# Score products of a gated linear recurrence in 32-column tiles instead of 128-column ones

## The chip, the cores and the metric

The kernel runs on one core of a Trainium2 chip. Time is device time in microseconds (us) of one execution; a lower time is better. The core has a matrix engine (TensorE, in the profile PE for the matmuls and PEld for the loads of the stationary operand), VectorE (DVE), ScalarE (ACT), GpSimd (POOL) and queues that start DMA transfers (SP among them). Each engine works through its own queue in order and waits on semaphores for the others. Matmul results land in PSUM, eight banks of 512 fp32 columns by 128 partitions, from where VectorE or ScalarE copies them to SBUF.

## What is computed

The reference is one layer of a decoder trunk for 1024 tokens plus 16 meta tokens, width 1024: a wide input projection, a gated linear recurrence in four heads, a causal pooling branch, a gated sum of both, an output projection, and a gated MLP. The part that matters here is the recurrence, cut to its core:

```python
def _hgrn2_chunk_step(state, xs):
    q, k, v, lf = xs
    b = jnp.cumsum(lf, axis=2)
    o_inter = jnp.einsum('bhtk,bhkv->bhtv', q * jnp.exp(b), state)
    diff = b[:, :, :, None, :] - b[:, :, None, :, :]
    ...
    decay = jnp.where(causal, jnp.exp(jnp.where(causal, diff, 0.0)), 0.0)
    scores = jnp.einsum('bhtk,bhtsk,bhsk->bhts', q, decay, k)
    o_intra = jnp.einsum('bhts,bhsv->bhtv', scores, v)
    ...
```

For every pair of tokens t >= s the score is a product over 128 channels in which each channel has its own decay exp(b[t] - b[s]). The decay can't be pulled out of the product for all pairs at once without overflow.

## The kernel before, in words

The kernel takes chunks of 128 tokens (`NCH` = 8 of them after the 16 meta tokens) and computes the 128 x 128 score matrix of a chunk by levels. A pair t > s is handled by the level `lv` of 2, 4, 8, 16, 32, 64 in which t lies in the right half and s in the left half of the same aligned block of 2 `lv` tokens: there the decay is split at the middle of the block into a factor for q and one for k, and a plain matmul gives the score. Pairs within two neighbouring tokens come from the "pair diagonal", a matmul of k and q with one more decay factor.

All of this is the generator `head_steps(h)` (lines 570 to 733), one per head, with channels on the partitions and tokens on the free axis:

- `level_in` (581 to 593) makes the tile `d` of a level: in each block the right half holds the scaled q, the left half the scaled k (VectorE or GpSimd at 587, 591, 592; ScalarE's exponentials at 589, 590).
- `level_mm` (595 to 613) multiplies. For levels 2 to 16 a chunk is one matmul (607): all 128 tokens of `d` are the stationary operand, the 64 tokens of the right halves move, and the result is 128 partitions by 64 columns, of which only the entries within a block count. For levels 32 and 64 there is one matmul per block (603), whose stationary operand is the left half (32 or 64 columns) and whose result lies at partition 2 `lv` i of the bank. Where 2 `lv` fits into the 16 meta tokens, a small matmul does those (612).
- `level_out` (615 to 631) brings the results into the score matrix `sc`. For levels 2 to 16 it is a masked copy per chunk on VectorE (627), with `masks[lv]` choosing the entries within blocks. For levels 32 and 64 plain copies (621).
- The levels go in pairs, (2, 4), (8, 16), (32, 64): the inputs of two levels, a `yield`, then the matmuls and the copies of both (lines 634 to 639).
- The pair diagonal (676 to 683): per chunk a matmul of 128 stationary k columns with 128 moving q columns (680) into two banks of four chunks, and a masked copy per chunk (683) with `mbase`. Line 685 does it for the meta tokens.
- After that come the states between chunks (692 to 703) and the outputs, which multiply `sc` with v (719).

All these matmuls are in fp32, and each such call shows in the trace as two weight loads and two MATMULs. The projections (`proj`, lines 164 to 178) split fp32 into two reduced-precision parts and use three matmuls instead.

What sets the order: the string `ORDER` (44 to 46) interleaves the projections of the four heads (F, Q, G), of the pooling branch (PV, PP) and of the branch outputs (BB, BA) with the steps of the heads (h0 to h3, one `yield` each). It is worked through at 981 to 1007. The list `POOLED` (47 to 49) gives some elementwise operations to GpSimd. In this stage the order within each engine's queue isn't written out by hand: it is decided when the kernel is built, by a planner that simulates the engines with its own costs (line 1523). The stages before it and most of the one after it are ordered by hand (`manual_schedule`). SBUF tiles of one token row come from 24 slots (`FM_SLOTS`), PSUM banks from a pool of eight.

Of the kernel before, what the change touches and what calls it, by code (L numbers as in the profile page):

```python
# [14 lines left out]
P = 128  # L15
D = 1024
SEQ = 1024
NM = 16
# [4 lines left out]
TQ = L - T0  # L23
CW = TQ // 3
HEADS = 4
NCH = 8
FF = 2816
KF = FF // P
# [28 lines left out]
def trunk_kernel(ctx: ExitStack, tc: tile.TileContext, x, meta_tokens, mix_norm_pre,  # L57
# [4 lines left out]
    act, dve, pool_e, pe = nc.scalar, nc.vector, nc.gpsimd, nc.tensor  # L62
# [21 lines left out]
    def nm(s):  # L84
        cnt[0] += 1
        return f"{s}_{cnt[0]}"

    def slot(n, dtype=F32, name="s"):
        return stage["fm", "p"].tile([P, n], dtype, tag="fm", name=nm(name), padded_shape=[P, L])
# [4 lines left out]
    def bank(name="ps"):  # L94
        return stage["ps", "p"].tile([P, 512], F32, tag="ps", name=nm(name))
# [11 lines left out]
    def small(shape, name, tag, bufs=4):  # L107
        return sm.tile(shape, F32, tag=tag, name=nm(name), bufs=bufs)
# [272 lines left out]
    CQ, CF, CI, CG, CV, CA, CB = 0, 512, 1024, 1536, 2048, 2560, 3584  # L381
    row_tiles = [(0, NM)] + [(NM + P * i, P) for i in range(NCH)]

# [19 lines left out]
    prow = slot(P, name="prow")  # L403
    NPR = 4 * KF + 3 * HEADS
    for at, n, src in ((0, 3 * KF, ffn_conv_w[0].rearrange("j (f p) -> (j f) p", p=P)),
                       (3 * KF, KF, ffn_conv_b[0].rearrange("(f p) -> f p", p=P)),
                       (4 * KF, HEADS, hgrn_lower_bounds[0].rearrange("(h p) -> h p", p=P)),
                       (4 * KF + HEADS, HEADS, hgrn_out_norm[0].rearrange("(h p) -> h p", p=P)),
                       (4 * KF + 2 * HEADS, HEADS, pool_scale[0].rearrange("(h p) -> h p", p=P))):
        nc.sync.dma_start(prow[at : at + n], src)  # L410
    par = const.tile([P, NPR], F32, name="par")
    cvw = par[:, : 3 * KF].rearrange("p (j f) -> p j f", j=3)
    cvb = par[:, 3 * KF : 4 * KF]
    lbt, ong, psc = (par[:, 4 * KF + i * HEADS : 4 * KF + (i + 1) * HEADS] for i in range(3))

    lb = const.tile([P, HEADS], F32, name="lb")
    oml = const.tile([P, HEADS], F32, name="oml")
# [80 lines left out]

    vd = dram.tile([NCH, P, 512], F32, name="vscr")
    vmeta = const.tile([P, 512], F32, name="vmeta")  # L500

    LEVELS = (2, 4, 8, 16, 32, 64)
    masks = {}
    mbase = const.tile([P, P], U8, name="mbase")
# [65 lines left out]
    def head_steps(h):  # L570
        q, kk, b, lf = (heads[h][z] for z in ("q", "kk", "b", "f"))
        heads[h]["v"] = slot(NCH * P, name="vh")
        nc.sync.dma_start(heads[h]["v"].rearrange("p (c v) -> p c v", c=NCH),
                          vd[:, :, h * P : (h + 1) * P].rearrange("c p v -> p c v"))
        sc = slot(NCH * P, name="sc")
        scm = small([NM, NM], "scm", "scm", 2)
# [17 lines left out]

        def level_mm(lv, qk):
            ps = bank("sl")
            half = lv >= 32
            for c in range(NCH):
                t = NM + c * P
                if half:  # L600
                    for i in range(P // (2 * lv)):
                        s, n = t + 2 * lv * i, 2 * lv * i
                        pe.matmul(ps[n : n + lv, c * lv : (c + 1) * lv], qk[:, s : s + lv], qk[:, s + lv : s + 2 * lv],
                                  start=True, stop=True)
                    continue
                rhs = qk[:, t : t + P].rearrange("p (b two h) -> p b two h", two=2, h=lv)[:, :, 1, :]
                pe.matmul(ps[:, c * 64 : (c + 1) * 64], qk[:, t : t + P], rhs, start=True, stop=True)
            pm = None
            if 2 * lv <= NM:
                pm = bank("sm")  # L610
                rhs = qk[:, :NM].rearrange("p (b two h) -> p b two h", two=2, h=lv)[:, :, 1, :]
                pe.matmul(pm[:NM, : NM // 2], qk[:, :NM], rhs, start=True, stop=True)
            return ps, pm

        def level_out(lv, ps, pm):
            if lv >= 32:
                o3 = sc.rearrange("p (c t) -> p c t", c=NCH)
                p3 = ps[:, : NCH * lv].rearrange("p (c h) -> p c h", c=NCH)
                for i in range(P // (2 * lv)):
                    n = 2 * lv * i  # L620
                    dve.tensor_copy(o3[n : n + lv, :, n + lv : n + 2 * lv], p3[n : n + lv])
                return
            o4 = sc.rearrange("p (c b two h) -> p c b two h", c=NCH, two=2, h=lv)[:, :, :, 1, :]
            p4 = ps.rearrange("p (c b h) -> p c b h", c=NCH, h=lv)
            m3 = masks[lv].rearrange("p (b h) -> p b h", h=lv)
            for c in range(NCH):
                dve.copy_predicated(o4[:, c], m3, p4[:, c])
            if pm is not None:
                dve.copy_predicated(scm.rearrange("p (b two h) -> p b two h", two=2, h=lv)[:, :, 1, :],
                                    masks[lv][:NM, : NM // 2].rearrange("p (b h) -> p b h", h=lv),  # L630
                                    pm[:NM, : NM // 2].rearrange("p (b h) -> p b h", h=lv))

        pend = []
        for pair in ((2, 4), (8, 16), (32, 64)):
            pend = [(lv, level_in(lv)) for lv in pair]
            yield
            outs = [(lv,) + level_mm(lv, d) for lv, d in pend]
            for o_ in outs:
                level_out(*o_)
# [26 lines left out]
        for j in range(2):  # L666
            pt = bank("pt")
            for i in range(4):
                t = NM + (4 * j + i) * P
# [3 lines left out]
        pe.transpose(pm[:NM, :P], kd[:, :NM], ident)  # L673
        ktm = small([NM, P], "ktm", "ktm", 2)
        act.copy(ktm, pm[:NM, :P])
        for j in range(2):
            ps = bank("sb")
            for i in range(4):
                t = NM + (4 * j + i) * P
                pe.matmul(ps[:, i * P : (i + 1) * P], kk[:, t : t + P], q[:, t : t + P], start=True, stop=True)  # L680
            for i in range(4):
                c = 4 * j + i
                dve.copy_predicated(sc[:, c * P : (c + 1) * P], mbase, ps[:, i * P : (i + 1) * P])
        pm = bank("sm")
        pe.matmul(pm[:NM, :NM], kk[:, :NM], q[:, :NM], start=True, stop=True)
        dve.copy_predicated(scm, mbase[:NM, :NM], pm[:NM, :NM])
# [4 lines left out]
        ps = bank("ds")  # L691
        pe.matmul(ps[:, :P], ktm, vmeta[:NM, h * P : (h + 1) * P], start=True, stop=True)
        act.copy(st[:, :P], ps[:, :P])
        for j in range(2):
            ps = bank("ds")
            cs = [c for c in range(4 * j, 4 * j + 4) if c < NCH - 1]
            for c in cs:
                i = c - 4 * j
                pe.matmul(ps[:, i * P : (i + 1) * P], kt[:, c * P : (c + 1) * P], V(c, h), start=True, stop=True)
            for c in cs:  # L700
                i = c - 4 * j
# [5 lines left out]
        o, rs = slot(TQ, name="o"), slot(TQ, name="rs")  # L707
# [6 lines left out]
        for j in range(2):  # L714
            ps = bank("po")
            for i in range(4):
                c = 4 * j + i
                t = NM + c * P
                pe.matmul(ps[:, i * P : (i + 1) * P], V(c, h), sc[:, c * P : (c + 1) * P], start=True, stop=False)
                pe.matmul(ps[:, i * P : (i + 1) * P], st[:, c * P : (c + 1) * P], qs[:, t : t + P],  # L720
                          start=False, stop=True)
# [3 lines left out]
        for lo, n in CH_Q:  # L725
            ps = bank("ms")
# [157 lines left out]
    with tc.manual_schedule(engines={E.Activation, E.DVE, E.PE}):  # L884
# [36 lines left out]
        for i in range(2, len(vtiles)):  # L921
            ps = bank("pv")
# [22 lines left out]
        for h in range(EARLY_G):  # L945
            src, n_k, xs, chunks, post = job("G", h)
            r = proj(None, 0, n_k, xs, chunks, ws=gl.next(), name="pg")
# [12 lines left out]
        for e in range(0, EARLY, 2):  # L960
            p = gates.start_pair(e)
# [343 lines left out]
    with tc.manual_schedule(engines={E.PE, E.Activation, E.DVE, E.Pool}):  # L1305
        for c in range(3):
            tiles_ = [pair("pm") for _ in range(3)]
            own = Rows(c, tiles_)
# [47 lines left out]
        p = [ffn.first(e) for e in range(EARLY)]  # L1356
# [171 lines left out]
```

## Time and profile before

| | |
|---|---|
| time, three runs | 1385.9, 1389.66, 1389.27 us; median 1389.27 |
| profiled execution, span from first to last instruction | 1388.5 us |
| instructions | 21566 |
| mean granted TensorE clock | 0.993 of full speed |
| matmuls of line 607 (levels 2 to 16), MATMULs | 256, from 287.3 to 437.5 us |
| matmuls of line 680 (pair diagonal), MATMULs | 64, from 352.5 to 479.8 us |
| masked copies of line 627 / 683 | 128 / 32 |

The profile gives for the profiled execution its span; the time of that execution with what lies around the span is not given separately, and the runs' times stand beside it. The page has the busy time of each engine, the span in 40 equal slices with the busy share in tenths, the DMA queues and the costliest groups of instructions. Other views answer questions: busy time in chosen stretches (optionally of one source line only), groups of instructions by line and shape with the mean length of one, who waited for whom, and a time line that merges equal neighbours. Matmuls are pipelined, so the lengths of successive MATMULs overlap, and what one costs the engine is the spacing between starts.

### The profile page before, as it was taken

The numbers are of one execution on the slowest core, as the hardware profiler recorded it, in microseconds if no ns is written. First come the engines' busy times: TensorE is split into PE (matmuls) and PEld (weight loads), VectorE is DVE, ScalarE is ACT, GpSimd is POOL, SyncE is SP. The second block draws the span as 40 slices with busy tenths as digits, with TensorE's granted clock in tenths as the row PEclk, the third lists the DMA queues.
The fourth block names the chain that finished last, engine by engine and source line by source line (L and its number), as shares of the span: only waits on it lengthen the run. The fifth ranks groups of instructions, "written<-read, shape, count | busy, mean of one in ns | idle before, by whom it ended". The sixth has DMA issues, their size and how long they took to land. (4 is left out here: it accounts for less than half of the span.)

```text
span 1388.5 us, 21566 instructions
## 1 busy us (share of the span) xinstructions
PE 1353.9 (98%) x8415; PEld 1225.2 (88%) x8415; DVE 961.7 (69%) x1397; ACT 564.5 (41%) x945; POOL 474.6 (34%) x357
## 2 busy tenths in 40 slices
PE   9999999999999999999987999999999999999997
PEld 7899999999999899987777788888999998788786
DVE  6764645389875755565589888888887777654557
ACT  5553333357554562136564322232222223543343
POOL 2015411237444610160037565534567652000100
PEclk9999999999999999999999999999999999999999
DMA  6134333321110024589842677665677889966524
GB/s 246 40 113 146 115 114 107 99 62 31 49 49 5 23 82 133 190 276 343 287 129 82 176 209 207 187 179 146 164 156 176 197 210 263 366 228 201 180 70 166
DMA packets 133220, 215.21 MB, mean 155 GB/s; under 512 B 8327, under 2 KB 76523, under 8 KB 133120
## 3 DMA queue, kind: packets, MB, share of 16 engines
q1 hardware_dynamic: 121056, 189.47, 40.4%
q0 software_dynamic: 12064, 24.38, 10.4%
q8 instruction: 66, 1.08, 0.3%
q14 instruction: 34, 0.28, 0.1%
HBM read 160.84 MB, written 76.05 MB: 171 GB/s over the span
## 5 line engine op out<-in xcount | busy, mean ns | idle before, releaser
L262 PE MATMUL P<-v,whi 128*128 128x258 f32 (+2 forms) x528 | 162.9, 322 | 7.0 <-DVE g L1227 4.5
L263 PE MATMUL P<-v,whi 128*128 128x258 f32 (+2 forms) x528 | 161.9, 321 | 0.0
L265 PE MATMUL P<-v,wlo 128*128 128x258 f32 (+2 forms) x528 | 141.0, 321 | 1.0 <-DVE wlo L210 1.0
L262 PEld LDWEIGHTS P<-v,whi 128*128 128x128 f32 x528 | 100.9, 191 | 15.5 <-DVE g L1227 4.9
L137 POOL TENSOR_TENSOR wlo<-wraw,whi 128x1024 fp32r<-128x1024 f32 (+2 forms) x23 | 50.0, 2173 | 183.6 <-ACT whi L136 101.8
L263 PEld LDWEIGHTS P<-v,whi 128*128 128x128 f32 x528 | 100.7, 191 | 7.6
L161 PE MATMUL pd<-rot 128*128 128x512 f32 x272 | 106.0, 390 | 0.3 <-DVE rot L1287 0.3
L162 PE MATMUL pd<-rot 128*128 128x512 f32 x272 | 105.9, 389 | 0.0
L136 ACT CAST whi<-wraw 128x1024 fp32r<-128x1024 f32 (+2 forms) x44 | 36.3, 825 | 148.1 <-PE pba L174 31.5
L265 PEld LDWEIGHTS P<-v,wlo 128*128 128x128 f32 x528 | 88.0, 190 | 8.8 <-DVE wlo L210 1.2
L209 ACT CAST whi<-wraw 128x512 fp32r<-128x512 f32 x90 | 53.0, 617 | 104.4 <-PE P L263 84.4
L210 DVE TENSOR_TENSOR wlo<-wraw,whi 128x512 fp32r<-128x512 f32 x82 | 75.7, 946 | 21.2 <-ACT whi L209 21.2
L1287 DVE TENSOR_TENSOR rot<-yt,rot 128x1024 fp32r<-128x1024 f32 x33 | 41.2, 1249 | 69.7 <-ACT rot L1286 69.7
L1171 POOL TENSOR_TENSOR ys<-y 128x512 f32<-128x512 f32 x22 | 35.2, 1599 | 143.7 <-issue 97.5
L235 POOL TENSOR_TENSOR swa<-wraw,wraw 128x512 f32<-128x512 f32 x30 | 45.1, 1503 | 96.4 <-DMA wraw<-in_w_in_dram 62.4
L160 PE MATMUL pd<-rot 128*128 128x512 f32 x272 | 72.8, 391 | 2.1 <-ACT rot L1286 2.1
L209 ACT CAST whi<-swa 128x512 fp32r<-128x512 f32 x60 | 35.8, 618 | 86.7 <-PE P L263 75.8
L1286 ACT CAST rot<-yt 128x1024 fp32r<-128x1024 f32 x33 | 34.6, 1051 | 89.2 <-PE pd L161 89.2
L1219 DVE SCALAR_TENSOR_TENSOR y<-g,par,y 128x1024 f32<-128x1024 f32 x44 | 65.7, 1494 | 0.7
L160 PEld LDWEIGHTS pd<-rot 128*128 128x128 f32 x272 | 50.8, 188 | 13.9 <-ACT rot L1286 3.4
L262 PE MATMUL P<-t2h,whi 128*128 128x258 f32 (+1 forms) x196 | 58.0, 312 | 3.7 <-ACT t2h L333 2.8
L209 ACT CAST whi<-swb 128x512 fp32r<-128x512 f32 x60 | 35.9, 619 | 63.2 <-PE P L263 62.4
(348 smaller groups left out, 4273.0 us busy)
## 6 DMA issues: line engine op xcount, KB each, us to landing
wraw<-in_w_in_dram SPq DMA_DIRECT2D x36, 512.0 KB
yt<-ysum SPq DMA_DIRECT2D x33, 512.0 KB
wraw<-in_ffn_w_gate_dram SPq DMA_DIRECT2D x26, 512.0 KB
wraw<-in_w_out_dram SPq DMA_DIRECT2D x24, 512.0 KB
wraw<-in_ffn_w_up_dram SPq DMA_DIRECT2D x22, 512.0 KB
wsum<-in_ffn_w_down_dram SPq DMA_DIRECT2D x22, 512.0 KB
ysum<-ys SPq DMA_DIRECT2D x11, 768.0 KB
sa<-sscr SPq DMA_DIRECT2D x16, 513.0 KB
```

The lines of the kernel that those rows point to most:

```text
L137: eng.tensor_tensor(lo, raw, rr(hi), ALU.subtract)
L160: pe.matmul(ps, ahi, bhi, start=first, stop=False)
L161: pe.matmul(ps, ahi, blo, start=False, stop=False)
L162: pe.matmul(ps, alo, bhi, start=False, stop=last)
L209: act.copy(hi, src)
L210: (pool_e if 4 <= i < 2 * self.early else dve).tensor_tensor(lo, src, rr(hi), ALU.subtract)
L235: pool_e.tensor_tensor(s1, a21, a22, ALU.add)
L262: pe.matmul(x[:, o : o + w], whi[:, k, :], xh[:, c : c + w], start=(k == 0), stop=False)
L263: pe.matmul(x[:, o : o + w], whi[:, k, :], xl[:, c : c + w], start=False, stop=False)
L265: pe.matmul(x[:, o : o + w], wlo[:, k, :], xh[:, c : c + w], start=False, stop=(k == 3))
L1219: dve.scalar_tensor_tensor(a, g[:, :, j : j + n], cvw[:, j, m : m + 1], a, ALU.mult, ALU.add)
L1287: dve.tensor_tensor(lo, src, rr(hi), ALU.subtract)
```

## The change

A constant `B` = 32 is added. For levels 2 to 16 and for the pair diagonal, each chunk of 128 tokens is cut into four blocks of 32, since no pair of these levels crosses a block of 32. Each block is its own matmul call: its 32 tokens are the stationary operand, and the moving operand is its 16 right-half tokens (levels) or its 32 tokens (diagonal). The result of block i lies at partitions 32 i to 32 i + 31, that is in the column tile i of the array, and the chunks stand next to each other: 16 columns per chunk for a level, 32 for the diagonal, which now takes one bank instead of two. The masked copies go per block position i, over all eight chunks at once: four copies per level, on 32 partitions and 8 x 16 elements each, and four for the diagonal, on 32 partitions and 8 x 32 elements. The mask of one chunk is broadcast over the chunks. Levels 32 and 64, the meta tokens and everything else stay.

```diff
-            half = lv >= 32
+            half = lv >= B
             for c in range(NCH):
                 t = NM + c * P
...
-                rhs = qk[:, t : t + P].rearrange("p (b two h) -> p b two h", two=2, h=lv)[:, :, 1, :]
-                pe.matmul(ps[:, c * 64 : (c + 1) * 64], qk[:, t : t + P], rhs, start=True, stop=True)
+                for i in range(P // B):
+                    own = qk[:, t + i * B : t + (i + 1) * B]
+                    rhs = own.rearrange("p (b two h) -> p b two h", two=2, h=lv)[:, :, 1, :]
+                    pe.matmul(ps[i * B : (i + 1) * B, c * B // 2 : (c + 1) * B // 2], own, rhs, start=True, stop=True)
...
-            for c in range(NCH):
-                dve.copy_predicated(o4[:, c], m3, p4[:, c])
+            n = B // 2
+            o6 = sc.rearrange("p (c i b two h) -> p c i b two h", c=NCH, i=P // B, two=2, h=lv)
+            p4 = ps[:, : NCH * n].rearrange("p (c b h) -> p c b h", c=NCH, h=lv)
+            for i in range(P // B):
+                r = slice(i * B, (i + 1) * B)
+                m4 = masks[lv][r, i * n : (i + 1) * n].rearrange("p (o b h) -> p o b h", o=1, h=lv)
+                dve.copy_predicated(o6[r, :, i, :, 1, :], m4.to_broadcast([B, NCH, n // lv, lv]), p4[r])
...
-        for j in range(2):
-            ps = bank("sb")
-            for i in range(4):
-                t = NM + (4 * j + i) * P
-                pe.matmul(ps[:, i * P : (i + 1) * P], kk[:, t : t + P], q[:, t : t + P], start=True, stop=True)
-            for i in range(4):
-                c = 4 * j + i
-                dve.copy_predicated(sc[:, c * P : (c + 1) * P], mbase, ps[:, i * P : (i + 1) * P])
+        ps = bank("sb")
+        for c in range(NCH):
+            for i in range(P // B):
+                own = slice(NM + c * P + i * B, NM + c * P + (i + 1) * B)
+                pe.matmul(ps[i * B : (i + 1) * B, c * B : (c + 1) * B], kk[:, own], q[:, own], start=True, stop=True)
+        for i in range(P // B):
+            r = slice(i * B, (i + 1) * B)
+            dve.copy_predicated(sc.rearrange("p (c i t) -> p c i t", c=NCH, i=P // B)[r, :, i, :],
+                                mbase[r, r].rearrange("p (o t) -> p o t", o=1).to_broadcast([B, NCH, B]),
+                                ps[r, : NCH * B].rearrange("p (c t) -> p c t", c=NCH))
```

More of the change, by code (lines that the diff above doesn't have):

```diff
@@ L25 @@
 HEADS = 4
+B = 32
 NCH = 8
@@ L615, in level_out @@
         def level_out(lv, ps, pm):
-            if lv >= 32:
+            if lv >= B:
                 o3 = sc.rearrange("p (c t) -> p c t", c=NCH)
@@ L622, in level_out @@
                 return
-            o4 = sc.rearrange("p (c b two h) -> p c b two h", c=NCH, two=2, h=lv)[:, :, :, 1, :]
-            p4 = ps.rearrange("p (c b h) -> p c b h", c=NCH, h=lv)
-            m3 = masks[lv].rearrange("p (b h) -> p b h", h=lv)
-            for c in range(NCH):
-                dve.copy_predicated(o4[:, c], m3, p4[:, c])
+            n = B // 2
[5 more added lines that the diff above has]
+                dve.copy_predicated(o6[r, :, i, :, 1, :], m4.to_broadcast([B, NCH, n // lv, lv]), p4[r])
             if pm is not None:
```

## The prediction

> **What bounds the kernel now.** I read the page's engine table and its slices first.
>
> ```profile
> span 1388.5 us, 21566 instructions
> ...
> PE 1353.9 (98%) x8415; PEld 1225.2 (88%) x8415; DVE 961.7 (69%) x1397; ACT 564.5 (41%) x945; POOL 474.6 (34%) x357
> ...
> PE   9999999999999999999987999999999999999997
> ...
> DVE  6764645389875755565589888888887777654557
> ```
>
> TensorE is busy for 98% of the span, without a dip from the ninth to the fourteenth slice (278 to 486 us), where the changed lines run. VectorE's digits stand at 8, 9, 8, 7 there first, then at 5. So I cut that part into two stretches, at the point where VectorE's load falls, and counted busy time in each.
>
> ```profile
> 283.00:372.00 89.00, 87.70 (x687) 85.98 (x686) 81.18 (x177) 53.33 (x81) 47.65 (x21) 1.00 0.14 43
> 372.00:483.00 111.00, 108.52 (x824) 104.97 (x823) 77.46 (x167) 56.88 (x96) 54.92 (x28) 0.98 0.09 27
> ```
>
> The columns are stretch, length, then PE, PEld, DVE, ACT and POOL busy with counts, then the granted clock. PE is idle for 1.30 us in the first stretch and 2.48 us in the second, so almost any PE work taken out shortens them, as long as nothing else then ends last. The candidate is DVE: it has 7.82 us to spare in the first stretch and 33.54 us in the second. What DVE waits for decides whether that room can be used. First stretch, all rows of its waits:
>
> ```profile
> DVE f L558 <- ACT f L557: 3.0, 2, 1.5
> DVE f L551 <- ACT f L546: 1.4, 2, 0.7
> DVE sc L627 <- PE sl L607: 1.1, 1, 1.1
> DVE wlo L137 <- ACT whi L136: 1.0, 1, 1.0
> DVE d L592 <- ACT d L590: 0.9, 1, 0.9
> DVE d L591 <- ACT d L589: 0.2, 1, 0.2
> ```
>
> Second stretch, its two longest:
>
> ```profile
> DVE sc L683 <- PE sb L680: 11.5, 3, 6.2
> DVE sc L627 <- PE sl L607: 8.5, 3, 7.0
> ```
>
> In the first stretch 6.5 us of DVE's waits are for ScalarE and 1.1 us for PE: DVE is close to a second bound there. In the second, 20.0 us are waits for the very matmuls that change: PE alone is the bound.
>
> **How much work is touched.** The matmuls of line 607 (levels 2 to 16) and 680 (pair diagonal), counted in the same two stretches:
>
> ```profile
> 283.00:372.00 89.00, 19.53 (x160) 18.81 (x160) 1.00 0.14 43
> 372.00:483.00 111.00, 11.68 (x96) 11.22 (x96) 0.98 0.09 27
> ```
>
> ```profile
> 283.00:372.00 89.00, 2.05 (x16) 1.86 (x16) 1.00 0.14 43
> 372.00:483.00 111.00, 5.85 (x48) 5.60 (x48) 0.98 0.09 27
> ```
>
> An fp32 matmul call shows as two weight loads with two MATMULs, so 16 MATMULs are one unit: one level, or the diagonal, of one head (8 chunks). There are 10 + 1 = 11 units in the first stretch and 6 + 3 = 9 in the second, 20 in all. After the change each unit has 8 x 4 = 32 calls, 64 MATMULs: 960 more in all.
>
> **The price of a MATMUL before and after.** Three bursts give it. Rows of a time line start with start and length; rows of groups end with busy time and mean length of one.
>
> ```profile
> 450.17 1.95 PE L680 MATMUL sb<-q,kk 128*128 128x128 f32 x16
> ```
>
> ```profile
> 322.29 0.18 PE L612 MATMUL sm<-d 128*16 128x8 f32 x1
> 322.30 0.22 PE L603 MATMUL sl<-d 128*32 128x32 f32 x1
> 322.33 0.17 PE L612 MATMUL sm<-d 128*16 128x8 f32 x1
> 322.35 0.67 PE L603 MATMUL sl<-d 128*32 128x32 f32 x31
> ```
>
> ```profile
> 323.12 0.98 PE L603 MATMUL sl<-d 128*64 128x64 f32 x14
> ```
>
> ```profile
> L680 PE MATMUL sb<-q,kk 128*128 128x128 f32 x64 | 7.9, 277 | 0.6 <-POOL kk L663 0.6
> L603 PE MATMUL sl<-d 128*64 128x64 f32 x64 | 4.6, 225 | 0.0
> L603 PE MATMUL sl<-d 128*32 128x32 f32 x128 | 2.9, 197 | 0.0
> ```
>
> A burst's length less its last matmul, over the number of steps, is the spacing. 128 columns: (1.95 - 0.277)/15 = 111.5 ns. 64 columns: (0.98 - 0.225)/13 = 58.1 ns. 32 columns: (0.67 - 0.197)/30 = 15.8 ns. From 128 to 64 columns the spacing halves; from 64 to 32 it falls to a quarter. The extra factor has a reason in the code: level 32 writes alternately to partitions 0 and 64, two column tiles, while level 64 writes to one. So one 32-column tile takes a matmul every 2 x 15.8 = 31.6 ns, and two run side by side. The L603 matmul that starts at 322.30, between the two halves of an L612 call, also says that a tile does not queue behind another tile's work.
>
> The change goes round four tiles. If all four run at once, the spacing is 31.6/4 = 7.9 ns; if no more than two do, it stays 15.8; without overlap it is 31.6. A unit costs 16 x 111.5 = 1.784 us before. After: 64 x 15.8 = 1.011 us (gain 0.773, for 20 units 15.5 us), 64 x 7.9 = 0.506 us (gain 1.278, in all 25.6 us), 64 x 31.6 = 2.022 us (loss 0.238, in all 4.8 us). The loss begins above 27.9 ns. No row shows four tiles. The nearest is the two-tile burst of 15.8, with the same kind of loop; overlap was full for two, so I take 12 ns, halfway towards four: 0.768 us a unit, a gain of 1.016, for 20 units 20.3 us of PE.
>
> [...]
>
> **Switching between tile widths.** Level 8's burst and the next unit of the same head:
>
> ```profile
> 303.07 1.89 PE L607 MATMUL sl<-d 128*128 128x64 f32 x16
> 304.89 0.21 PE L612 MATMUL sm<-d 128*16 128x8 f32 x2
> 305.03 0.32 PE L607 MATMUL sl<-d 128*128 128x64 f32 x1
> ```
>
> From 303.07 to 305.03 is 1.96 us, 0.18 more than a unit: the two narrow L612 matmuls and the way into and out of their width. When the neighbours are narrow too, some of the twelve such visits (levels 2, 4, 8 of four heads) lose it. Between 0 and 12 x 0.18 = 2.2 us; I take 1 us, as a change of width stays at each end of a burst.
>
> **VectorE.** Eight copies per unit become four, with as many elements per partition altogether (4 x 128 for a level, 4 x 256 for the diagonal).
>
> ```profile
> 351.17 1.13 DVE L627 COPY_PREDICATED sc<-mask,sl 128x64 f32<-128x64 uint8 x8
> 357.50 1.68 DVE L683 COPY_PREDICATED sc<-mbase,sb 128x128 f32<-128x128 uint8 x8
> ```
>
> 1.13/8 = 141 ns for 64 elements and 1.68/8 = 210 ns for 128: 1.08 ns an element and 72 ns fixed. Four fixed costs less is 0.29 us a unit, 5.8 us in all, 3.2 of them in the first stretch. That four copies use 32 partitions each saves nothing; if the longer pattern cost more per element, this saving goes, so 0 to 5.8. The copies of a unit wait for its last matmul as now. The diagonal takes one PSUM bank instead of two; no wait of this part is for a bank of it, so nothing is priced. The new instructions are fetched too (packets, MB, share of 16 DMA engines):
>
> ```profile
> q8 instruction: 66, 1.08, 0.3%
> ```
>
> 21566 instructions took 66 packets, so 1920 more take 6, at 0.003 x 16 x 1388.5/66 = 1 us each. They lie beside running matmuls and I price them at nothing; were each waited for, 6 us.
>
> **The sum.** Second stretch: 9 x 1.016 = 9.1 us; I count 9. First stretch: PE offers 11 x 1.016 = 11.2 us. DVE then needs 81.18 - 3.2 + its 6.5 us of waits for ScalarE = 84.5 of 89, which allows 4.5 us if nothing is rearranged; PE can run ahead with projections that wait for no head, so the truth is between 4.5 and 11.2, and I take 6.5, nearer the lower as in-order queues stop at the first step that is late. With 1 us of switching, 16.5 us. The profiled span of 1388.5 becomes 1372. The page gives no time around the span; the median of the runs is 1389.27, 0.77 higher, and they differ by 3.8, so I add 0.77: about 1373. This case by itself reaches from 4.5 + 9 x 0.773 = 11.5 us to 25.6 + 1 us: 1362.7 to 1377.8.
>
> **Rivals.**
> VectorE sets the pace, in the first stretch fully and in part of the second. For it: 81.18 of 89 us. Against: 20 us of DVE's waits in the second are for the matmuls that shrink. It gives 4.5 us, and half of 9 x 0.773 = 7.0: 8 us, so 1381.
>
> The gain is lost to order. Outside the blocks ordered by hand, a planner decides each engine's queue at build time, and it will see other lengths. The longest PE wait here now:
>
> ```profile
> PE ppv L173 <- ACT st L693: 2.5, 1, 2.5
> ```
>
> Six or seven more waits of 2.5 us take all 16.5: 1389. Against it: four heads' steps now cost PE 1.30 + 2.48 = 3.78 us of idle time altogether.
>
> Slower: the matmuls cannot be issued that fast. The 15.8 ns burst is 32 MATMULs long, behind slow ones during which the sequencer could fill the queue; now 64 and, for a pair of levels, 128 stand in a row. If the sequencer settles at the 58.1 ns of the 64-column burst, a unit costs 3.72 us, and 20 cost 38.7 us more: 1428; at 31.6 ns it is 1394, with the six fetches up to 1400. It decides from 27.9 ns on; just short of that, at 25 ns, a unit would cost 1.6 us and the whole would come to 1385.6. Against it: right after that burst 14 matmuls of 64 columns still came every 58.1 ns, half of what 128 columns take, so the array and not the sequencer set their pace. [...]
>
> That the four tiles give no more than two is not a rival but the lower half of my case.
>
> **Chances.** Forecast 0.53, VectorE's pace 0.20, lost to order (or a spacing of about 25 ns) 0.13, issue-bound beyond 27.9 ns 0.14, half of it at 1394 to 1400. A measurement of this kernel can tell about 0.3%, 4.2 us, from no change. The first two cases are faster, with 0.02 of the third: 0.75; within: 0.11; slower: 0.14. The range goes from 1362, all four tiles and nothing lost, to 1390, which takes in the lost gain; it leaves out the slower case and a little below.
>
> **What would show it.** MATMULs of the level line: 1024 of 32 columns in place of 256, in bursts of 64 or 128 spaced 8 to 16 ns; PE busy time in this part down by some 15 to 25 us; DVE's copies at about 0.21 us and half as many; the second stretch shorter by about 9 us and the first by 4 to 11, with DVE over 90% busy in it; everything after it as before, only earlier. Wrong: a spacing above 28 ns, or PE idle time that grows by as much as its work shrinks.

## The result and the profile after

After: median 1378.72 us of four runs (1375.45 to 1380.77), beside 1389.47 us (1385.9 to 1389.81) of the kernel before. The ratio is 0.9928, 95% interval 0.991 to 0.9945: 7.6 to 12.5 us faster. The predicted time was 1373 in a range of 1362 to 1390, so the direction and the range held, and the gain was 46 to 76% of the 16.5 us expected. The profiled execution took 1380.77 us with a span of 1379.1, 1.7 us lying around it; its span is 9.4 us shorter than before's.

The same lines of the page as before: span, busy times, TensorE's and VectorE's slices, instruction fetches.

```profile
span 1379.1 us, 23409 instructions
...
PE 1334.7 (97%) x9375; PEld 1204.7 (87%) x9375; DVE 964.0 (70%) x1317; ACT 564.8 (41%) x945; POOL 472.1 (34%) x357
...
PE   9999999998999999999988999999999999999997
...
DVE  6764645389887655555589898787878776744557
...
q8 instruction: 74, 1.21, 0.3%
```

TensorE's busy time fell by 1353.9 - 1334.7 = 19.2 us. Its idle time, span less busy time, rose from 34.6 to 44.4 us, by 9.8. The difference, 9.4 us, is what the span gained: half of what TensorE saved came back as waiting. TensorE's tenth slice now shows an 8 (310 to 345 us), where VectorE's shows a 9. The two stretches of the prediction, moved to where that work now lies (length, then PE, PEld, DVE, ACT, POOL busy, then the clock):

```profile
283.00:370.00 87.00, 76.53 (x1195) 73.64 (x1194) 80.55 (x126) 52.92 (x80) 44.55 (x21) 0.92 0.15 45
370.00:480.00 110.00, 106.54 (x1309) 102.22 (x1308) 83.45 (x140) 60.91 (x101) 55.42 (x28) 0.98 0.10 30
```

TensorE is idle for 10.47 us in the first and 3.46 in the second, where it was 1.30 and 2.48. The clock in the first fell from 1.00 to 0.92. Where the time was won is seen from two marks. The first is the first output matmul of head 0 (its row has start and length); the row under it counts all the work ahead of it. Before:

```profile
375.00 0.39 PE L712 MATMUL po<-scm,vmeta 16*128 16x16 f32 x2
```

```profile
0.00:375.00 375.00, 371.38 (x2682) 355.09 (x2683) 243.18 (x451) 174.14 (x311) 115.94 (x99) 1.00 0.32 102
```

After:

```profile
375.65 0.39 PE L719 MATMUL po<-scm,vmeta 16*128 16x16 f32 x2
```

```profile
0.00:375.65 375.65, 362.86 (x3210) 345.53 (x3210) 246.57 (x407) 173.99 (x311) 112.95 (x99) 0.98 0.32 102
```

The 528 MATMULs more are those of the eleven units ahead of the mark (704 in place of 176), so the work is the same. TensorE was busy for 8.5 us less and waited 9.2 us longer: 12.79 in place of 3.62. By then nothing was won. The changed matmuls ahead of the mark fell by more than 8.5 us. They took 19.53 us (levels) and 2.05 us (diagonal) before, the 160 and 16 MATMULs of the prediction's first stretch. After, levels and then diagonal:

```profile
0.00:375.65 375.65, 7.47 (x640) 6.93 (x640) 0.98 0.32 102
```

```profile
0.00:375.65 375.65, 0.76 (x64) 0.65 (x64) 0.98 0.32 102
```

That is 13.35 us less. So TensorE's other matmuls, the same in number, took 13.35 - 8.52 = 4.8 us longer, where the granted clock in the stretch from 283 us on was 0.92 instead of 1.00. Waiting took 9.2 us of the 13.35 and the slower other matmuls 4.8; together that is all of it.

The second mark is the last matmul of the diagonal (shortest, median and longest in ns, then first and last start). Before:

```profile
L680 PE MATMUL sb<-q,kk x64: 275/275/378, 352.5 to 479.9; 128*128 128x128 f32 x64
```

After:

```profile
L685 PE MATMUL sb<-q,kk x256: 196/196/217, 352.1 to 471.3; 128*32 128x32 f32 x128
```

There it was 8.6 us. So between the two marks 9.2 us were won, and the stretch before the first gave none. The level and diagonal matmuls themselves, groups of the stretch 270 to 490 us after (busy time, mean ns, then idle time before them and its cause):

```profile
L610 PE MATMUL sl<-d 128*32 128x16 f32 x1024 | 11.5, 189 | 5.2 <-DVE d L593 4.7 <-ACT qs L648 0.5
L685 PE MATMUL sb<-q,kk 128*32 128x32 f32 x256 | 3.1, 199 | 0.3 <-POOL kk L668 0.3
```

Together 14.6 us, and 5.5 us of waiting. What they mostly wait for is the tile `d` that VectorE makes, 4.7 us; that is just under half of TensorE's 10.47 us in the first stretch, and the longest of its other waits there, 2.2 us, is for ScalarE. Time line of TensorE after, a burst that did not wait, and one that did:

```profile
286.95 0.70 PE L610 MATMUL sl<-d 128*32 128x16 f32 x62
```

```profile
317.82 1.06 PE L610 MATMUL sl<-d 128*32 128x16 f32 x64 [3.64 <-DVE d L593]
```

The first gives a spacing of (0.70 - 0.189)/61 = 8.4 ns. The second, the same kind of burst, is half as long again: it follows 3.64 us of idleness, and the granted clock there is 0.50, as two short stretches show.

```profile
316.00:318.00 2.00, 0.18 (x12) 0.18 (x16) 2.00 (x3) 1.99 (x6) 2.00 (x2) 0.92 0.00 0
318.00:320.00 2.00, 2.00 (x146) 2.00 (x144) 2.00 (x1) 1.88 (x3) 2.00 (x2) 0.50 0.04 8
```

In the first of these VectorE, ScalarE and GpSimd are busy nearly throughout and TensorE is not: the inputs of the levels are late.

Last, VectorE's masked copies after (groups as above):

```profile
L632 DVE COPY_PREDICATED sc<-mask,sl 32x128 f32<-32x128 uint8 x64 | 21.3, 332 | 5.7 <-PE sl L610 4.2
L688 DVE COPY_PREDICATED sc<-mbase,sb 32x256 f32<-32x256 uint8 x16 | 7.1, 443 | 5.0 <-PE sb L685 4.0 <-PE sm L692 0.8
```

Before:

```profile
L627 DVE COPY_PREDICATED sc<-mask,sl 128x64 f32<-128x64 uint8 x128 | 19.6, 247 | 9.6 <-PE sl L607 9.5
L683 DVE COPY_PREDICATED sc<-mbase,sb 128x128 f32<-128x128 uint8 x32 | 7.0, 296 | 11.5 <-PE sb L680 11.5
```

Half as many copies took 28.4 us in place of 26.6.

### The profile page after: what moved, and what is told of

Same layout as the page of the kernel before. It is cut to its first block, busy times and chain, and to the rows that moved or that the text cites. A ratio compares the mean times of both kernels' runs of the same rounds, so it can differ in the third digit from the quotient of the medians.

```text
span 1379.1 us, 23409 instructions
## 1 busy us (share of the span) xinstructions
PE 1334.7 (97%) x9375; PEld 1204.7 (87%) x9375; DVE 964.0 (70%) x1317; ACT 564.8 (41%) x945; POOL 472.1 (34%) x357
## 5 line engine op out<-in xcount | busy, mean ns | idle before, releaser
L1293 ACT CAST rot<-yt 128x1024 fp32r<-128x1024 f32 x33 | 34.6, 1052 | 93.1 <-PE pd L162 93.1
L211 DVE TENSOR_TENSOR wlo<-swb,whi 128x512 fp32r<-128x512 f32 x60 | 56.8, 952 | 8.3 <-ACT whi L210 8.3
```

The costliest lines, as they stand in the source:

```text
L211: (pool_e if 4 <= i < 2 * self.early else dve).tensor_tensor(lo, src, rr(hi), ALU.subtract)
```

## The experiments

Three explanations for the missing part of the gain were tested. V: VectorE's queue became the bound, and its masked copies are what would have to shrink. O: the planner, which orders each engine's queue when the kernel is built, lost it by its new order. P, formed after the first four runs: the bound is the elementwise work that makes the level inputs, on VectorE and GpSimd together, not the copies by themselves. Each ratio is to the kernel before on the same chip, with its 95% interval. The last three columns are from the page of one profiled execution of each kernel, where TensorE's idle time is the span less its busy time; for z3 that execution was the fastest of five, for x3 the slowest of ten:

| kernel | median us | ratio (interval) | span | PE busy | PE idle |
|---|---|---|---|---|---|
| before | 1389.47 | | 1388.5 | 1353.9 | 34.6 |
| after | 1378.72 | 0.9928 (0.991 to 0.9945) | 1379.1 | 1334.7 | 44.4 |
| x1, wide, no masked copies | 1386.92 | 0.9989 (0.9978 to 1.0) | 1385.2 | 1351.0 | 34.2 |
| x2, narrow, no masked copies | 1380.22 | 0.9935 (0.9921 to 0.995) | 1378.4 | 1330.5 | 47.9 |
| x3, one tile after the other | 1385.81 | 0.9981 (0.997 to 0.9991) | 1387.2 | 1353.2 | 34.0 |
| x4, compact copies, merged by GpSimd | 1379.94 | 0.9934 (0.9919 to 0.9949) | 1376.2 | 1329.2 | 47.0 |
| y1, wide, no multiplications | 1386.24 | 0.9992 (0.9982 to 1.0002) | 1384.6 | 1352.0 | 32.6 |
| y2, narrow, no multiplications | 1368.93 | 0.987 (0.9853 to 0.9886) | 1366.5 | 1330.1 | 36.4 |
| y3, narrow, GpSimd relieved | 1385.08 | 0.9978 (0.9968 to 0.9988) | 1384.9 | 1331.9 | 53.0 |
| y4, y3 with compact copies | 1369.14 | 0.9867 (0.9853 to 0.9882) | 1367.0 | 1327.6 | 39.4 |
| z1, y4 with one step on GpSimd | 1367.61 | 0.985 (0.9835 to 0.9865) | 1364.9 | 1325.3 | 39.6 |
| z2, wide, GpSimd relieved, fewer copies | 1389.62 | 1.0004 (0.9994 to 1.0014) | 1388.8 | 1354.5 | 34.3 |
| z3, levels alone narrow | 1384.89 | 0.9964 (0.9949 to 0.9979) | 1378.9 | 1332.3 | 46.6 |
| z4, diagonal alone narrow | 1387.14 | 0.9988 (0.9978 to 0.9997) | 1385.9 | 1350.3 | 35.6 |

### The masked copies taken away, x1 and x2

x1 is before without the copies of lines 627 and 683, x2 is after without those of 632 and 688.

```diff
-            for c in range(NCH):
-                dve.copy_predicated(o4[:, c], m3, p4[:, c])
...
-            for i in range(4):
-                c = 4 * j + i
-                dve.copy_predicated(sc[:, c * P : (c + 1) * P], mbase, ps[:, i * P : (i + 1) * P])
```

```diff
-            for i in range(P // B):
-                r = slice(i * B, (i + 1) * B)
-                m4 = masks[lv][r, i * n : (i + 1) * n].rearrange("p (o b h) -> p o b h", o=1, h=lv)
-                dve.copy_predicated(o6[r, :, i, :, 1, :], m4.to_broadcast([B, NCH, n // lv, lv]), p4[r])
...
-        for i in range(P // B):
-            r = slice(i * B, (i + 1) * B)
-            dve.copy_predicated(sc.rearrange("p (c i t) -> p c i t", c=NCH, i=P // B)[r, :, i, :],
-                                mbase[r, r].rearrange("p (o t) -> p o t", o=1).to_broadcast([B, NCH, B]),
-                                ps[r, : NCH * B].rearrange("p (c t) -> p c t", c=NCH))
```

> The kernel before, with the masked copies of levels 2 to 16 and of the pair diagonal left out (the scores keep only the blocks of levels 32 and 64). Theory V (VectorE's queue sets the pace in the first stretch, 283 to 370 us, once the matmuls are short): VectorE loses about 26 us of busy time, but with wide matmuls PE is the bound nearly everywhere (3.8 us idle in both stretches before), so at most 4 us faster: 1385 to 1389. Theory O (the changed kernel lost its gain to the planner's new order of the queues, VectorE's load decides nothing): the same here, 1385 to 1392.

> The changed kernel with the same masked copies left out. Theory V: without the copies' load on VectorE the matmuls' gain of about 25 us comes through, 20 to 25 us below the wide kernel without copies: 1361 to 1367, PE idle in 283 to 480 us under 7 us. Theory O: the gain stays near 10 us: 1375 to 1380, PE idle there about 13 us as in the changed kernel.

x1 came out at 0.9989 and x2 at 0.9935, no faster than after. V falls in its simple form: 28.4 us of copies less for VectorE, and nothing won. TensorE's idle time in the two stretches was 17.5 us, where V expected under 7. The two stretches of x2:

```profile
283.00:370.00 87.00, 77.84 (x1222) 75.03 (x1221) 78.41 (x94) 53.14 (x80) 46.52 (x21) 0.96 0.15 45
370.00:480.00 110.00, 101.71 (x1278) 97.50 (x1277) 70.90 (x91) 60.73 (x101) 54.09 (x28) 0.97 0.10 30
```

VectorE is still busy for 78.41 us of the first, 2.1 less than after. Its other operations had become longer. x2's time line of VectorE shows one of them, a multiplication of two SBUF operands:

```profile
308.06 2.34 DVE L593 TENSOR_TENSOR d<-d,kk 128x512 f32<-128x512 f32 x1
```

GpSimd worked at the same time:

```profile
303.62 6.24 POOL L588 TENSOR_TENSOR d<-b 128x1040 f32<-128x1040 f32 x1 [8.54 <-DVE b L561]
```

The shortest such multiplications take 0.67 us (below, y4). So the next runs had to vary that work and not the copies.

### Tile after tile, x3

The same calls as after, with the loops turned: all eight chunks of one column tile, then the next.

```diff
-        for c in range(NCH):
-            for i in range(P // B):
+        for i in range(P // B):
+            for c in range(NCH):
```

The same for the levels.

> The changed kernel with the loops over block positions and chunks exchanged, so that eight calls in a row go to one column tile. The instructions and their number are the same, only their order differs. If four tiles run side by side in the change (spacing about 8 ns) and one tile takes a matmul every 31.6 ns, a unit of 64 MATMULs goes from 0.53 to 2.0 us, 20 units 30 us more of PE work; the PE idle time of the changed kernel (about 13 us in this part) hides some of it: 1390 to 1400. If the gain comes from elsewhere (fewer columns loaded, not side-by-side tiles), the time stays at 1377 to 1381.

It ran at 1385.81 us (0.9981), 7 us slower than after; the expected loss was larger, 1390 to 1400. Time line and group of x3:

```profile
287.46 1.80 PE L612 MATMUL sl<-d 128*32 128x16 f32 x61
```

```profile
L612 PE MATMUL sl<-d 128*32 128x16 f32 x1024 | 28.9, 184 | 1.1 <-ACT qs L650 0.6 <-DVE d L593 0.5
```

The spacing is (1.80 - 0.184)/60 = 26.9 ns against 8.4, and the level matmuls take 28.9 us against 11.5. So after's spacing does come from tiles that run side by side: the order of the calls alone is worth a factor of 3.2 in the spacing. It also measures what TensorE's time is worth here: 18.5 us more of busy time (1353.2 against 1334.7) cost 7.1 us at the median (8.1 us of span), since TensorE's idle time fell by 10.4 to 34.0. Less than half of what TensorE saves reaches the end.

### Compact copies, merged by GpSimd, x4

One masked copy per level on all 128 partitions, into a compact tile of 8 x 32 columns, and at the end of a head four copies on GpSimd that put it into `sc`. Heads 0 and 2 share one compact tile, so a part of head 0's scores is lost.

```diff
+        scd = junk[:, (h % 2) * NCH * B : (h % 2 + 1) * NCH * B]
+        pool_e.memset(scd, 0.0)
...
+            o4 = scd.rearrange("p (c b two h) -> p c b two h", c=NCH, two=2, h=lv)[:, :, :, 1, :]
...
-            for i in range(P // B):
...
+            m4 = bmasks[lv].rearrange("p (o b h) -> p o b h", o=1, h=lv)
+            dve.copy_predicated(o4, m4.to_broadcast([P, NCH, n // lv, lv]), p4)
...
-            dve.copy_predicated(sc.rearrange("p (c i t) -> p c i t", c=NCH, i=P // B)[r, :, i, :],
...
+            pool_e.tensor_copy(sc.rearrange("p (c i t) -> p c i t", c=NCH, i=P // B)[r, :, i, :], scd3[r])
```

> The narrow matmuls as in the change, but one masked copy per level and per diagonal, on all 128 partitions, into a compact tile of 256 columns; GpSimd brings the compact blocks into the score matrix, four copies per head. VectorE's copies go from 80 (28 us) to 20 (about 5 us). Theory V: most of the matmuls' gain comes through, as without copies: 1361 to 1369, and PE idle time in this part under 8 us. Theory O: as the changed kernel, 1375 to 1380.

0.9934, as after. With a quarter of the copies nothing was won either: the second run that speaks against V. The merges went to the engine that was to be suspected next: x4's four per head stand in its groups as

```profile
L700 POOL COPY sc<-junk 32x256 f32<-32x256 f32 x16 | 10.3, 644 | 3.3 <-DVE scm L703 2.8
```

### The multiplications taken away, y1 and y2

Both leave out the multiplications of the scaled q and k in levels 2 to 16 (lines 592 and 593 after); those of levels 32 and 64 stay. y1 does it in before, y2 in after.

```diff
+            if lv < 32:
+                return d
```

> The kernel before with the multiplications by q and k left out of the inputs of levels 2 to 16 (32 elementwise operations of VectorE and GpSimd fewer; the products multiply the decay factors alone). Theory P: once the matmuls are short, the first stretch waits for the level inputs, whose elementwise operations on VectorE and GpSimd read two SBUF operands and hold each other up, so that both engines' load counts as one. Here PE is still the bound: 1383 to 1389. Theory O (planner's new order): also 1383 to 1389.

> The changed kernel with the same 32 multiplications left out. Theory P: VectorE and GpSimd together lose 25 to 35 us of busy time in this part, PE's idle time there falls below 6 us, and the gain over the wide kernel without them is 18 to 25 us: 1360 to 1368. Theory O: the gain stays at about 10 us: 1374 to 1380.

y1 is at 0.9992, within the uncertainty of before; y2 at 0.987, 17 us faster than y1 and 8 to 10 faster than after (by the ratios and by the medians). That is just short of what P expected of it. The queues of y2 are ordered by the same planner as those of after, so O alone doesn't explain why the gain appears here; P does. But leaving out multiplications also shortens the chain of steps ahead of each matmul, which y2 can't tell from the load on the two engines. The first stretch of y2:

```profile
283.00:370.00 87.00, 81.60 (x1250) 79.00 (x1249) 67.78 (x123) 55.86 (x85) 33.50 (x16) 0.96 0.15 45
```

VectorE went from 80.55 to 67.78 us, GpSimd from 44.55 to 33.50, TensorE's idle time from 10.47 to 5.40. With 3.43 in the second stretch that makes 8.8 us, where P expected under 6.

### GpSimd relieved, y3, and with compact copies, y4

y3 keeps only the weight splits in GpSimd's list (all of them, where the expectation speaks of two projections; the other 27 operations, the level inputs among them, go back to VectorE). y4 does that and takes the compact copies of x4, merged by ScalarE, with a tile of its own for head 2, so that nothing is lost.

```diff
-POOLED = ("e1k.0 e1k.3 kdmul.2 kdmul.3 kdsub.2 lk32.1 lk4.1 lk64.0 lq16.1 lq16.3 lq32.0 lq32.1 lq32.2 lq4.0 "
-          "lq64.0 lq64.3 lq8.0 lq8.1 lq8.2 osg.2 qsmul.2 qsmul.3 sub2.2 sub32.1 sub4.1 sub8.1 sub8.3 wBA2 wBA6 "
+POOLED = ("wBA2 wBA6 "
```

```diff
-            pool_e.tensor_copy(sc.rearrange("p (c i t) -> p c i t", c=NCH, i=P // B)[r, :, i, :], scd3[r])
+            act.copy(sc.rearrange("p (c i t) -> p c i t", c=NCH, i=P // B)[r, :, i, :], scd3[r])
```

> The changed kernel with all elementwise operations of the heads on VectorE; GpSimd keeps its share of the weight splits of two branch projections. Theory P: an operation takes about half as long on VectorE as on GpSimd and VectorE's others are no longer stretched, so nothing is lost, or up to 5 us gained: 1374 to 1381, with the operation of line 588 at 1.2 us instead of 1.4 to 1.7. Rival (GpSimd really works beside VectorE): VectorE gets 12 to 20 us more work where it was 93% busy: 1386 to 1394.

> As the run before (all elementwise work of the heads on VectorE), and one masked copy per level and diagonal on 128 partitions into a compact tile, which ScalarE brings into the score matrix with four copies per head. VectorE's masked copies go from 28 us to about 5. Theory P: with GpSimd quiet VectorE's own time is what counts, so the copies matter now: 6 to 15 us below the run before, 1364 to 1374. If copies never matter: as the run before.

y3 missed: 0.9978, 6 us slower than after. GpSimd's share of the work was of some use after all while the copies fill VectorE. y4 is at 0.9867, 19 us faster than before and 8 to 10 faster than after. So the two measures interact: with GpSimd's list as it was, compact copies give nothing (1378.72 to 1379.94); with it emptied of all but the weight splits, 16 us (1385.08 to 1369.14). The first pair differs in one thing more, since x4 has the merges on GpSimd and y4 on ScalarE; but x2, without copies and without merges, came out the same as x4. A reason shows when equal groups are compared. After, VectorE's level inputs (stretch 270 to 490 us):

```profile
L588 DVE TENSOR_TENSOR d<-b 128x1024 f32<-128x1024 f32 x11 | 18.1, 1665 | 0.1
L588 DVE TENSOR_TENSOR d<-b 128x1040 f32<-128x1040 f32 x8 | 10.4, 1316 | 0.1
L593 DVE TENSOR_TENSOR d<-d,kk 128x520 f32<-128x520 f32 x11 | 10.4, 941 | 0.8 <-ACT d L591 0.8
L593 DVE TENSOR_TENSOR d<-d,kk 128x512 f32<-128x512 f32 x10 | 9.0, 906 | 0.2
L592 DVE TENSOR_TENSOR d<-d,q 128x520 f32<-128x520 f32 x8 | 8.8, 1095 | 1.1 <-ACT d L590 1.1
...
L592 DVE TENSOR_TENSOR d<-d,q 128x512 f32<-128x512 f32 x5 | 3.9, 771 | 0.1
```

y4, the same groups, and its compact copies:

```profile
L597 DVE TENSOR_TENSOR d<-b 128x1024 f32<-128x1024 f32 x12 | 17.5, 1484 | 0.0
L597 DVE TENSOR_TENSOR d<-b 128x1040 f32<-128x1040 f32 x12 | 14.5, 1230 | 0.1
L601 DVE TENSOR_TENSOR d<-d,q 128x512 f32<-128x512 f32 x12 | 9.8, 819 | 3.2 <-ACT d L599 3.2
L601 DVE TENSOR_TENSOR d<-d,q 128x520 f32<-128x520 f32 x12 | 8.3, 690 | 2.0 <-ACT d L599 2.0
L602 DVE TENSOR_TENSOR d<-d,kk 128x520 f32<-128x520 f32 x12 | 8.2, 687 | 0.0
L602 DVE TENSOR_TENSOR d<-d,kk 128x512 f32<-128x512 f32 x12 | 8.1, 676 | 0.0
...
L639 DVE COPY_PREDICATED junk<-bmask,sl 128x128 f32<-128x128 uint8 x12 | 3.9, 327 | 1.8 <-PE sl L619 1.8
```

After, VectorE did 53 of these operations in 60.6 us, with 19 on GpSimd. In y4 it did all 72 in 66.4 us. In x2, with the copies gone, the same 53 took 70.4 us, more than all 72 in y4. So the 19 on GpSimd spare VectorE only 5.8 us, because the operation that VectorE runs meanwhile is held up. A pair of rows from after shows it; VectorE, then GpSimd:

```profile
314.32 1.76 DVE L592 TENSOR_TENSOR d<-d,q 128x520 f32<-128x520 f32 x1
```

```profile
312.55 2.98 POOL L592 TENSOR_TENSOR d<-d,q 128x512 f32<-128x512 f32 x2
```

0.69 us, the mean of this form in y4, became 1.76. The masked copies did not suffer so: their mean was 332 ns after and 330 in y3, where GpSimd had only its weight splits. That is part of why taking them out of after (x2) did not help: they ran beside GpSimd unhindered, and without them the 53 operations took 9.8 us longer. Why the other 18.6 us of the 28.4 brought nothing is not shown. Why the multiplications, with both inputs in SBUF, were held up and the masked copies, whose data come from PSUM, were not, is not shown either: no run varied where the inputs lie.

In y4 the page's TensorE has the same 9375 MATMULs as after but 7.1 us less busy time, and the first stretch fits that:

```profile
283.00:370.00 87.00, 80.48 (x1252) 77.77 (x1251) 73.86 (x124) 57.56 (x88) 16.19 (x7) 0.98 0.15 45
```

The clock is 0.98 where it was 0.92. Where the matmuls behind a wait of TensorE run at half the clock, as the burst at 317.82 us did (granted clock 0.50, 1.06 us in place of 0.70), the wait costs more than its length.

### One step back on GpSimd, z1

In y4 TensorE's longest wait was 3.6 us for the diagonal's k; z1 gives the multiplication of head 0's k for the diagonal back to GpSimd.

```diff
-POOLED = ("wBA2 wBA6 "
+POOLED = ("e1k.0 wBA2 wBA6 "
```

> The compact masked copies with ScalarE's merging and the heads' elementwise work on VectorE, but head 0's k factor for the pair diagonal back on GpSimd. In the version without it PE's longest wait was 3.6 us for exactly that operation on VectorE. Theory P: GpSimd holds up VectorE's two-operand work only while it runs, about 2 us, so one operation that stands alone on the way to the diagonal pays: 1 to 4 us below the version without it, 1365 to 1369. Rival (any GpSimd work there costs as much as it saves): 1368 to 1371.

1367.61 us (0.985): the fastest version, some 21 us faster than before and 11 than after. Against y4 the 1.5 us lie within the intervals, and the wait only changed its name:

```profile
PE sb L694 <- DVE q L676: 3.7, 1, 3.7
```

### The same relief with wide matmuls, z2

Before with GpSimd's list cut as in y3, one copy of 512 elements per level and two for the diagonal.

```diff
-            for c in range(NCH):
-                dve.copy_predicated(o4[:, c], m3, p4[:, c])
+            m4 = masks[lv].rearrange("p (o b h) -> p o b h", o=1, h=lv)
+            dve.copy_predicated(o4, m4.to_broadcast([P, NCH, 64 // lv, lv]), p4)
```

> The kernel before, with its wide matmuls, VectorE relieved in the same way: the heads' elementwise work off GpSimd, and the masked copies gathered into one per level and two per diagonal (512 elements each). Control for the compact version: if its gain of 19 us comes from the narrow matmuls, which show once VectorE is relieved, then relief alone gives the wide kernel next to nothing, PE staying the bound: 1384 to 1391. If the relief itself is the gain: below 1380.

1.0004 (0.9994 to 1.0014): nothing. Before, TensorE is the bound, and relief of VectorE is worth nothing by itself, as x1 and y1 said. The 19 us of y4 need both, the narrow matmuls and the relief of VectorE and GpSimd.

### Levels alone and diagonal alone, z3 and z4

z3 puts line 680's wide diagonal back into after, z4 the wide levels.

```diff
-        for c in range(NCH):
-            for i in range(P // B):
-                own = slice(NM + c * P + i * B, NM + c * P + (i + 1) * B)
-                pe.matmul(ps[i * B : (i + 1) * B, c * B : (c + 1) * B], kk[:, own], q[:, own], start=True, stop=True)
...
+            for i in range(4):
+                t = NM + (4 * j + i) * P
+                pe.matmul(ps[:, i * P : (i + 1) * P], kk[:, t : t + P], q[:, t : t + P], start=True, stop=True)
```

```diff
-                for i in range(P // B):
-                    own = qk[:, t + i * B : t + (i + 1) * B]
...
+                rhs = qk[:, t : t + P].rearrange("p (b two h) -> p b two h", two=2, h=lv)[:, :, 1, :]
+                pe.matmul(ps[:, c * 64 : (c + 1) * 64], qk[:, t : t + P], rhs, start=True, stop=True)
```

> The change for levels 2 to 16 alone; the pair diagonal as before. 16 of the 20 units become short, 10 of them in the first stretch, where VectorE with GpSimd decides, and 6 in the second, where PE is the bound. Theory P: about 6 x 1.25 us plus 0 to 2 us: 5 to 9 us, 1379 to 1384.

> The change for the pair diagonal alone. 4 of the 20 units, 3 of them in the second stretch. Theory P: 3 x 1.25 us plus up to 1 us: 2.5 to 5 us, 1384 to 1387, nearly the same per unit as PE's work that it saves, while the levels give less than half of theirs.

z3: 0.9964 (0.9949 to 0.9979), 3 to 7 us; z4: 0.9988 (0.9978 to 0.9997), 0.4 to 3 us. Both medians lie just past what was expected. Theory P had expected of the diagonal nearly all that it saves TensorE, about 1.25 us for each of its units; 0.4 to 3 us for four units is 0.1 to 0.8 each, so that did not come. The two gains add to some 5 to 7 us where both together give about 10, but the intervals leave room for a plain sum (7 + 3); no interaction is shown.

## Why the prediction was right, and where it was off

**The price of a MATMUL.** Taken at 12 ns between 7.9 and 15.8; measured 8.4. Four column tiles run side by side; the price without that is not 31.6 ns but 26.9 (x3), of which full overlap would give 6.7. The level and diagonal matmuls fell from 31.2 + 7.9 us (groups of lines 607 and 680 before) to 14.6, by 24.5, more than the 20.3 of the sum:

```profile
L607 PE MATMUL sl<-d 128*128 128x64 f32 x256 | 31.2, 275 | 0.2 <-DVE d L592 0.2
```

**The rival that ends slower**, matmuls that can't be issued fast enough, is refuted: 8.4 ns over 62 MATMULs in a row. No run shows the spacing of about 25 ns that the chances set beside the lost order: across tiles it was 8.4 ns, and only within one tile do x3's 26.9 ns lie near it.

**Second stretch.** 9 us were counted; 9.2 came between the two marks. The wait was judged rightly, but the number is in part luck: the changed matmuls saved 24.5 - 13.35 = 11.2 us there, not 9.1, and 2.0 of it did not arrive.

**First stretch: the step that failed.** "PE can run ahead with projections that wait for no head, so the truth is between 4.5 and 11.2, and I take 6.5". It gave nothing: at head 0's outputs after stands 0.65 us later than before. The prediction's own sign of being wrong, idle time of TensorE that grows by as much as its work shrinks, came true there (8.5 us less work, 9.2 more waiting), though not in the second stretch. The lower bound of 4.5 was itself too high, for two reasons. It let VectorE's work shrink by 3.2 us, where VectorE's busy time ahead of the first mark grew by 3.4 (243.18 to 246.57), which takes away all of the 4.5. And it held VectorE's other operations at their lengths of before; x2 and y4 show that these lengths depend on GpSimd (53 level inputs took 70.4 us in x2 and all 72 took 66.4 in y4). A third loss had no term in the sum at all: beside TensorE's new waits the clock was 0.92, and its other matmuls took 4.8 us longer. One reading was off as well: after 8, 9, 8, 7 VectorE's digits before are 5 and 7, not only 5; the sum rests on the two stretches and not on them.

**VectorE's copies.** "0 to 5.8" us saved; measured 1.8 us lost (26.6 to 28.4). The failed term is the overlap of copies that follow each other. Before, eight copies of 64 elements took 1.13 us, 141 ns each, though their mean length is 247: they overlapped. After, time line of VectorE:

```profile
307.85 1.28 DVE L632 COPY_PREDICATED sc<-mask,sl 32x128 f32<-32x128 uint8 x4
```

1.28/4 = 320 ns each, with a mean length of 332 over all: hardly any overlap. Each of the four starts on another group of 32 partitions. Before's diagonal copies, also of 128 elements but all on the same 128 partitions, came every 210 ns at a mean length of 296. No run changed the group and nothing else, so that the change of group is what costs the overlap is an estimate from these two rows. The prediction's 72 ns fixed and 1.08 ns an element were read off overlapping copies and gave 210 ns for 128 elements, where it takes 320; so the 0.21 us expected of each copy was wrong too.

**"VectorE sets the pace"**, the rival at 1381, was the nearest to what was measured in the first stretch, and right about where; about the cause it was half right. Less of VectorE's own load alone gave nothing (x2, x4); it took less work in the level inputs (y2), or a relief of VectorE and GpSimd together (y4), which hold each other up: a multiplication on VectorE took 0.69 us in y4 and 1.76 beside GpSimd (after), and a subtraction on GpSimd (line 588, 1040 elements) 2.49 us after and 6.24 in x2.

**"Lost to order"** does not explain it by itself: y2 and y4 go through the same planner and gain 18 to 19 us. No run gave after's operations to VectorE and GpSimd in another order, so how much a better order alone would win back stays open. The six more instruction packets became eight (66 to 74), and no wait of TensorE's is for one.

**Switching between tile widths.** No run shows the 1 us that was added for it by itself.

**What stays open.** The split of the missing gain into waiting and slower matmuls (9.2 and 4.8 us ahead of the first mark) is read off one profiled execution; no run held the clock fixed. From after to y4 the pages give 5.0 us less idle time and 7.1 us less busy time. Theory P's own forecast of y3 was wrong in sign, so how much GpSimd should take has only been tried at three points.

## What to carry to other kernels

A saving on the engine that is busy 98% of the time counts only as far as the inputs from the other engines are early: here half of 19 us came back as waiting, and the next change had to be made on VectorE and GpSimd, where it had been worth nothing before (z2). The busy times of two engines that hold each other up can't be added or traded one for one; compare the length of one operation alone and beside the other engine (here 0.69 and 1.76 us) before giving work away. And copies that go round partition groups lost their overlap here: one every 320 ns at a mean length of 332. One copy over all 128 partitions in their place was worth nothing by itself (x4) and 16 us once GpSimd had been relieved (y3 to y4).

## What the runs showed of the hardware

- Matmuls of 32 stationary columns that go round four column tiles came every 8.4 ns (after, x62, no gap), and 26.9 ns apart when eight calls in a row went to one tile (x3).
- A VectorE multiplication with two SBUF inputs of 512 elements took 0.68 us in the mean in y4, where GpSimd had little to do, and one took 2.34 us beside GpSimd (x2); a subtraction of GpSimd's own of 1040 elements took 6.24 us there.
- After a gap of 3.64 us of TensorE, the granted clock was 0.50 from 318 to 320 us, and a burst that had taken 0.70 us took 1.06 (after).
- Masked copies on changing groups of 32 partitions hardly overlapped: 320 ns each for 128 elements, four in a row, at a mean length of 332 (after). Where all used the same 128 partitions, eight in a row took 141 ns each for 64 elements and 210 for 128, at mean lengths of 247 and 296 (before).
